# Weight sums of the first down part's twelve seven-product units: from VectorE sums staged in SBUF to accumulating transfers in HBM, with two signs turned

## The chip, the cores and the metric

The kernel runs on one core of one Trainium2 chip. The metric is the device time of one execution in microseconds (us). Before the change three runs took 1453.7, 1454.1 and 1455.69 us; the median is 1454.1 us.

## The reference

One decoder layer on 256 tokens of width 2048, all in float32: a mixer of two gated attention branches, then a gated feed-forward block with a short causal convolution. What matters here are the banded (sliding-window) attention of the mixer and the last product of the feed-forward block:

```python
s = jnp.einsum('bnqhgd,bnkhd->bhgnqk', q, kb) * SWA_HEAD_DIM ** -0.5     # banded attention, 32 query heads
s = jnp.where(mask, s + bias, -jnp.inf)                                  # bias by head and distance
...
def conv_ffn(h, w_up, conv_w, conv_b, w_down):                           # w_up 2048 x 11264, w_down 5632 x 2048
    a, b = jnp.split(h @ w_up, 2, axis=-1)
    ap = jnp.pad(a, ((0, 0), (CONV_WIDTH - 1, 0), (0, 0)))
    c = conv_b
    for j in range(CONV_WIDTH):
        c = c + conv_w[j] * ap[:, j:j + S]
    return (jax.nn.gelu(c, approximate=True) * b) @ w_down
```

## The kernel before, in words

**Products.** Every weight arrives by a transfer on SP's queue as a raw tile of 128x1024 float32 (512 KB), is split by ACT (line 163) and DVE (line 164) into a high and a low part, `whi` and `wlo`, and enters three matmuls (`mm3`, lines 197 to 200: high times high, high times low, low times high). A raw tile feeds twelve matmuls. Raw tiles and parts stand in rings of a few buffers; while a conversion is late, TensorE has only the parts already made.

**Seven-product units.** `pair_gemm` (line 273) makes a product over 1024 columns. Its letters "p" are plain units, its letters "s" units in which eight block products are replaced by seven (Strassen's scheme in Winograd's form, for two weight rows of 128, `even` and `odd`, and two halves of 512 columns). Such a unit needs four sums of weight blocks and four sums of token blocks (`token_sums`, line 375). With E0, E1 the halves of the even row and O0, O1 those of the odd row, the weight sums are E1-E0, O1-E1, then O1-(E1-E0), and O0 minus that.

**Parked sums.** `park_sums` (line 237) makes these sums early: `load` brings the two weight rows into SBUF by two transfers on POOL's queue (line 245), `even` and `odd` are four DVE subtractions of 128x512 (line 252), and two more POOL transfers store the result into two HBM tiles `td` (lines 257 and 262). `seven_parked` (line 300) later loads these tiles on SP's queue as if they were weights. `park_a` (line 269) is its use for the first down part (the first 24 of the 44 weight rows of 128, over both halves of the columns): `PAIR_ORDER` holds six "s" for each of the two products, twelve units in all, with tiles named `ta0` to `ta11` (in the profile `ta_s` in SBUF, `ta` in HBM). Four of them (`EARLY`, line 836) are made during the gate and output products behind the banded attention, eight (line 1376) during the up products. The same helper makes sums for other products (`tw`, `tb`, `tc`); these are not touched.

**Order of the work.** `at(t, f)` files a step under tick t and `tick()`, which the product loops call once for each raw tile or two, runs the steps that are due. The program text so made is then put in order for each engine by a scheduler, before the run; on the chip every engine and every transfer queue takes its instructions in that fixed order. POOL issues its transfers itself, so a POOL instruction that waits holds up all POOL instructions behind it.

**Banded attention.** From line 706 on, 16 units of two heads each go through the ticks, two ticks apart (`swa_unit`, line 625), between the matmuls of the projection of the queries. Unit u needs its bias tile, which POOL fetches out of a small HBM strip (line 633, two buffers: unit u's fetch waits until unit u-2 has used its own), at the DVE step of line 644, which adds it to the scores in PSUM. At the unit's end POOL makes the low part of the output (line 698). The tick counter is set to 0 just before (line 584). The first product of the kernel (`first_product`, line 501, about the first 50 us) comes ahead of it.

Of the kernel before, what the change touches and what calls it, by code (L numbers as in the profile page):

```python
# [11 lines left out]
F32 = mybir.dt.float32  # L12
# [4 lines left out]
ALU = mybir.AluOpType  # L17
# [25 lines left out]
def trunk_layer(ctx, tc, x, x_cols_in, conv_cols_in, g_mix_post, g_ffn_post, w_in, w_q, w_kv,  # L43
# [193 lines left out]
    def park_sums(name, w, k, c0, pl, tag, t0, bufs=None):  # L237

        td = [dram.tile([P, 1024], F32, name=f"{name}{i}") for i in range(2)]
        st = []  # L240

        def load():
            st.append(sb(pl, [P, D], f"{name}s", tag=tag, bufs=bufs))
            for i in range(2):
                ins = pool.dma_start(st[0][:, i * 1024:(i + 1) * 1024], w[(k + i) * P:(k + i + 1) * P, c0:c0 + 1024])
                if tag not in staged:
                    tc.keep_in_program_order(ins)
            staged.add(tag)

        def less(o, x, y):  # L250
            o, x, y = (st[0][:, i * 512:(i + 1) * 512] for i in (o, x, y))
            tc.keep_in_program_order(vec.tensor_tensor(o, x, y, op=ALU.subtract))

        def even():
            less(0, 1, 0)
            less(1, 3, 1)
            pool.dma_start(td[0], st[0][:, 0:1024])

        def odd():
            less(3, 3, 0)  # L260
            less(2, 2, 3)
            pool.dma_start(td[1], st[0][:, 1024:2048])

        at(t0 - 5, load)
        at(t0, even)
        at(t0 + 1, odd)
        return td

    def park_a(i, pl, tag, t0, **kw):
        u, p = (i, 0) if i < NA[0] else (i - NA[0], 1)  # L270
        return park_sums(f"ta{i}_", w_down, 2 * u, 1024 * p, pl, tag, t0, **kw)

    def pair_gemm(name, w, k0, c0, order, act_of, s_of, kind, d, place=None, sums=None, parked=None, held=None, into=None):

        c11, c12, c21, c22 = c = banks(kind, f"c{name}_")
        q, used = [], set()
        row = lambda k: w[(k0 + k) * P:(k0 + k + 1) * P, c0:c0 + 1024]
        half = lambda w_, i: tuple(x[:, i * 512:(i + 1) * 512] for x in w_)

        def mul(o, x, w_, last=False):  # L280
            mm3(o, *x, *w_, id(o) not in used, last)
            used.add(id(o))

        chunks, hold = [2 * order.count("p")], len(held) if held else 0
        left = [order.count("s")]

        def plain(u, last):
            for k in (2 * u, 2 * u + 1):
                chunks[0] -= 1
                w_ = convert(raw_row(row(k)), 1024, into=into(chunks[0]) if hold else None)  # L290
                for t in range(NT):
                    if t and chunks[0] < hold:
                        held[hold - 1 - chunks[0]] = (act_of(k, 1), w_)
                        continue
                    for j in range(2):
                        mul(c[2 * t + j], act_of(k, t), half(w_, j),
                            not (chunks[0] or (t and hold)) and (j == 1 or not left[0]))
                tick()

        def seven_parked(u, last):  # L300
            s1, s2, s3, s4 = s_of(u)
            if not q:
                q[:] = banks(1 - kind, f"q{name}_")
            q1, q5, q7, q6 = q
            w_ = convert(raw_row(row(2 * u + 1)), 1024)
            mul(c11, act_of(2 * u + 1, 0), half(w_, 0))
            mul(c12, s4, half(w_, 1))
            w_ = convert(raw_row(row(2 * u)[:, 0:512], 512), 512)
            mul(q1, act_of(2 * u, 0), half(w_, 0), last)
            w_ = convert(raw_row(parked[u][0]), 1024)  # L310
            mul(q5, s1, half(w_, 0), last)
            mul(q7, s3, half(w_, 1), last)
            tick()
            w_ = convert(raw_row(parked[u][1]), 1024)
            left[0] -= 1
            mul(q6, s2, half(w_, 1), last)
            mul(c21, act_of(2 * u + 1, 1), half(w_, 0))
            tick()
            if last:
                end_sums()  # L320

        def seven(u, last):
            s1, s2, s3, s4 = s_of(u)
            even, odd = place()
            pool.dma_start(even, row(2 * u))
            pool.dma_start(odd, row(2 * u + 1))
            ta, tb = sums()
            w_ = convert(odd, 1024)
            weight_sums(even, odd, ta, tb)
            if not q:  # L330
                q[:] = banks(1 - kind, f"q{name}_")
            q1, q5, q7, q6 = q
            mul(c11, act_of(2 * u + 1, 0), half(w_, 0))
            mul(c12, s4, half(w_, 1))
            w_ = convert(even, 512)
            mul(q1, act_of(2 * u, 0), half(w_, 0), last)
            w_ = convert(ta, 1024)
            mul(q5, s1, half(w_, 0), last)
            mul(q7, s3, half(w_, 1), last)
            tick()  # L340
            w_ = convert(tb, 1024)
            left[0] -= 1
            mul(q6, s2, half(w_, 0), last)
            mul(c21, act_of(2 * u + 1, 1), half(w_, 1))
            tick()
            if last:
                end_sums()

        def end_sums():
            q1, q5, q7, q6 = q  # L350
            d0, d1, d2, d3 = d() if callable(d) else d

            def first_sums():
                act.copy(d0, q1)
                vec.tensor_tensor(d1, d0, q6, op=ALU.add)
                vec.tensor_tensor(d2, d1, q7, op=ALU.add)

            def more_sums():
                vec.tensor_tensor(d3, d2, q5, op=ALU.add)
                vec.tensor_tensor(d1, d1, q5, op=ALU.add)  # L360

            at(now[0], first_sums)
            at(now[0] + 1, more_sums)

        n = order.count("s")
        plain_of, seven_of = iter(range(n, len(order))), iter(range(n))
        for i, kd_ in enumerate(order):
            if kd_ == "s":
                u = next(seven_of)
                (seven_parked if parked else seven)(u, u == n - 1)  # L370
            else:
                plain(next(plain_of), i == len(order) - 1)
        return c

    def token_sums(g, a, m, hi, lo):

        vec.tensor_tensor(a, g[:, 0:512], g[:, 512:1024], op=ALU.add)
        a11, a21, a12, a22 = (a[:, i * P:(i + 1) * P] for i in range(4))
        m1, m2, m3, m4 = (m[:, i * P:(i + 1) * P] for i in range(4))
        vec.tensor_tensor(m1, a21, a22, op=ALU.add)  # L380
        vec.tensor_tensor(m3, a11, a21, op=ALU.subtract)
        vec.tensor_tensor(m2, m1, a11, op=ALU.subtract)
        vec.tensor_tensor(m4, a12, m2, op=ALU.subtract)
        split_to(hi, lo, m)
        return [[x[:, i * P:(i + 1) * P] for x in (hi, lo)] for i in range(4)]

# [205 lines left out]
    OH, OL = pair_view(highs(ot)), pair_view(lows(ot))  # L592
    sb(base, [P, LINE_W], "line_w")

    qx_of, xs_of = {}, {}

    def swa_q(g, acc):
# [235 lines left out]
    out_b(0, tb[0], (pss, "s"))  # L833
    tb[1], tb[2] = gate_pair(1)
    parked_b2 = []
    parked_a = [park_a(i, pg, "gr", now[0] + 5 + 5 * i, bufs=2) for i in range(EARLY)]
    out_b(1, tb[1], (pss, "s"))
    tb[3] = gate_b(3)
    out_b(2, tb[2])
# [485 lines left out]
    def g_sums(u):  # L1325

        if u % 2 == 0:
            s_tiles[u // 2] = sums_tile("s", u // 2)
        hi, lo = (s_tiles[u // 2][:, (u % 2) * 1024 + i * 512:(u % 2) * 1024 + (i + 1) * 512] for i in range(2))
        a, m = (sb(s_pool[0], [P, 512], f"s{n}{u}", tag="hx", bufs=2) for n in "am")  # L1330
        s_of[u] = token_sums(gtiles[u].bitcast(F32), a, m, hi, lo)

    def gemm_cols(acc, c0):

# [37 lines left out]
            at(now[0] + 1 + 2 * i, lambda i=i: conv_cols(4 * c + i, sa[0][i], sa[1][i], slot0 + i))  # L1372

    es7 = ffn_up0()
    for i in range(sum(NA) - EARLY):
        parked_a.append(park_a(i + EARLY, t0=now[0] + 8 + 15 * i // 2, **STAGE))
    for c in range(1, 6):
        if c == 2:
            for i in range(8):
# [25 lines left out]
    for p in range(2):  # L1405
        d = [dsum[t][2 * p + j] for t in range(NT) for j in range(2)]
        c = pair_gemm(f"d{p}", w_down, 0, 1024 * p, PAIR_ORDER[p], lambda k, t: (GH(k)[:, t * P:(t + 1) * P], GL(k)[:, t * P:(t + 1) * P]),
                      lambda u: s_of[u], p, d, parked=parked_a[NA[0] * p:])
        for n_, (o, x_) in enumerate(zip(d, c)):
            at(now[0] + n_, lambda o=o, x_=x_: vec.tensor_tensor(o, o, x_, op=ALU.add))  # L1410
    more_raw.clear()
    turn.update(raw=0)
    sb_tiles = []
# [153 lines left out]
NB2 = B2_ORDER.count("s")  # L1567
W_ORDER = "ppspspsp"
PAIR_ORDER = ("pppspsspsssp", "ppspspsspssp")
EARLY = 4  # L1570
NA = [o.count("s") for o in PAIR_ORDER]
NB_ = B_ORDER.count("s")
XCUT = [0, 1, 2, 3, 4, 6, 8, 10, 12, 14, 16]
# [67 lines left out]
```

## Time and profile before

| What | Value |
|---|---|
| median of three runs | 1454.1 us |
| the profiled execution: its own time, its span | 1454.23 us, 1452.5 us |
| PE busy | 1442.0 us (99%) |
| DVE busy | 1160.4 us (80%) |
| POOL busy | 118.2 us (8%) |
| share of the 16 DMA engines taken by SP's queue, by POOL's queue | 59.8%, 15.0% |
| mean rate of all transfers | 248 GB/s |
| granted TensorE clock | 0.998 |

PE is TensorE's matmuls, PEld its weight loads, DVE VectorE, ACT ScalarE, POOL GpSimd, SP SyncE. Times in the views are microseconds from the start of the span. Matmuls overlap each other, so that "busy" says that TensorE has work, not how much of it; how long an engine waited for which other one stands in the view of waits. The first queue in the list of transfers (q1) is SP's, q0 is POOL's.

### The profile page before, as it was taken

Reading aid. Unit: us, or ns where it says so; the run is one execution under the profiler, and the core shown is the slowest. Engines: PE = TensorE matmul, PEld = TensorE weight load, DVE = VectorE, ACT = ScalarE, POOL = GpSimd, SP = SyncE. Lnnn points to the kernel's source line nnn. Section 1 sums busy time; section 2 is a strip of 40 time slices with the busy share of each in tenths; the row PEclk is TensorE's granted clock in tenths of the full one; section 3 lists DMA queues with packets and bytes.
Section 4 is the critical chain, followed back from the end, with each engine's and each line's share of the span. In section 5 each row is a group of like instructions: output and inputs, shape, how many; then the busy total and the mean of one; then the engine's idle time right before and its main releaser. Section 6 shows DMA issues by size and latency. Waiting matters only on the chain.

```text
span 1452.5 us, 21438 instructions
## 1 busy us (share of the span) xinstructions
PE 1442.0 (99%) x7518; PEld 1233.7 (85%) x7518; DVE 1160.4 (80%) x2056; ACT 864.7 (60%) x1422; POOL 118.2 (8%) x222
## 2 busy tenths in 40 slices
PE   9999999999999999999999999999999999999997
PEld 7888888888898888888888888888888888888886
DVE  7788896766878775888789899876777797987798
ACT  7588864544555655546566565655646565555673
POOL 2022110010000001100000111000000101000000
PEclk9999999999999999999999999999999999999999
DMA  8655376699875759965666898866878888789965
GB/s 309 209 171 163 103 261 188 219 327 294 244 220 178 230 164 319 348 232 183 219 205 208 272 331 288 292 206 210 310 276 262 312 276 292 246 265 309 340 219 203
DMA packets 164684, 359.69 MB, mean 248 GB/s; under 512 B 20816, under 2 KB 31952, under 8 KB 164576
## 3 DMA queue, kind: packets, MB, share of 16 engines
q1 hardware_dynamic: 143152, 282.49, 59.8%
q0 software_dynamic: 21280, 75.56, 15.0%
q8 instruction: 59, 0.97, 0.3%
q14 instruction: 49, 0.40, 0.1%
q10 hardware_dynamic: 144, 0.26, 0.1%
HBM read 323.62 MB, written 34.65 MB: 247 GB/s over the span
## 4 chain that ended last, share of the span: by engine, by line
PE 91%; DVE 4%; ACT 2%; DMA 2%; issue 1%; SPq 0%; DVEq 0%; ACTq 0%
PE ub L1340 10%; PE ua L1340 9%; PE accg L200 9%; PE accg L198 9%; PE accg L199 9%; PE ub L1344 5%; PE ua L1344 5%; PE cd L199 2%; PE cd L198 2%; PE cd L200 2%; DVE wlo L164 2%; DMA raw<-in_ffn_w_up_dram 1%; PE cdc L199 1%; PE cdc L198 1%; PE cdc L200 1%
## 5 line engine op out<-in xcount | busy, mean ns | idle before, releaser
L163 ACT CAST whi<-raw 128x1024 fp32r<-128x1024 f32 (+2 forms) x497 | 504.0, 1023 | 373.9 <-PE accg L200 109.1
L164 DVE TENSOR_TENSOR wlo<-raw,whi 128x1024 fp32r<-128x1024 f32 (+2 forms) x497 | 585.0, 1188 | 172.0 <-ACT whi L163 165.6
L198 PE MATMUL accg<-whi,ahl 128*128 128x512 f32 (+1 forms) x416 | 162.5, 391 | 0.0
L200 PE MATMUL accg<-whi,ahl 128*128 128x512 f32 (+1 forms) x416 | 160.7, 386 | 0.0
L199 PE MATMUL accg<-wlo,ahl 128*128 128x512 f32 (+1 forms) x416 | 159.8, 384 | 0.0
L1340 PE MATMUL ub<-ahl,whi 128*128 128x512 f32 x640 | 154.7, 391 | 0.2 <-DVE uu L1239 0.2
L1340 PE MATMUL ua<-ahl,whi 128*128 128x512 f32 x640 | 154.6, 391 | 0.0
L1340 PEld LDWEIGHTS ub<-ahl,whi 128*128 128x128 f32 x640 | 117.5, 188 | 23.1 <-ACT cc L1232 0.5
L1340 PEld LDWEIGHTS ua<-ahl,whi 128*128 128x128 f32 x640 | 117.6, 188 | 22.7
L198 PE MATMUL accg<-whi,bhl 128*128 128x512 f32 x256 | 100.8, 394 | 0.0
L200 PE MATMUL accg<-whi,bhl 128*128 128x512 f32 x256 | 100.0, 391 | 0.0
L199 PE MATMUL accg<-wlo,bhl 128*128 128x512 f32 x256 | 99.9, 390 | 0.0
L200 PEld LDWEIGHTS accg<-whi,ahl 128*128 128x128 f32 x416 | 78.1, 188 | 15.2
L199 PEld LDWEIGHTS accg<-wlo,ahl 128*128 128x128 f32 x416 | 78.3, 188 | 13.0
L198 PEld LDWEIGHTS accg<-whi,ahl 128*128 128x128 f32 x416 | 78.2, 188 | 12.9
L1344 PEld LDWEIGHTS ub<-ahl,wlo 128*128 128x128 f32 x640 | 82.2, 191 | 3.3
L1344 PEld LDWEIGHTS ua<-ahl,wlo 128*128 128x128 f32 x640 | 82.2, 191 | 3.1
L1344 PE MATMUL ua<-ahl,wlo 128*128 128x256 f32 x640 | 83.7, 283 | 0.0
L1344 PE MATMUL ub<-ahl,wlo 128*128 128x256 f32 x640 | 83.3, 283 | 0.0
L200 PEld LDWEIGHTS accg<-whi,bhl 128*128 128x128 f32 x256 | 48.1, 188 | 10.1
L199 PEld LDWEIGHTS accg<-wlo,bhl 128*128 128x128 f32 x256 | 48.1, 188 | 9.6
L198 PEld LDWEIGHTS accg<-whi,bhl 128*128 128x128 f32 x256 | 48.1, 188 | 9.6
(659 smaller groups left out, 2679.7 us busy)
## 6 DMA issues: line engine op xcount, KB each, us to landing
raw<-in_ffn_w_up_dram SPq DMA_DIRECT2D x142, 512.0 KB, 4.9
raw<-in_w_in_dram SPq DMA_DIRECT2D x105, 512.0 KB, 4.6
raw<-in_ffn_w_down_dram SPq DMA_DIRECT2D x66, 512.0 KB, 5.6
xraw<-in_ffn_w_up_dram SPq DMA_DIRECT2D x34, 512.0 KB, 5.2
raw<-in_w_o_swa_dram SPq DMA_DIRECT2D x32, 512.0 KB, 5.3
raw<-in_w_o_mla_dram SPq DMA_DIRECT2D x26, 512.0 KB, 6.9
raw<-in_w_out_dram SPq DMA_DIRECT2D x26, 512.0 KB, 4.6
ta_s<-in_ffn_w_down_dram POOLq DMA_DIRECT2D x24, 512.0 KB, 5.9
```

The costliest lines, as they stand in the source:

```text
L163: act.copy(hi[:, a:b], raw[:, a:b])
L164: vec.tensor_tensor(lo[:, a:b], raw[:, a:b], hi[:, a:b].bitcast(F32), op=ALU.subtract)
L198: pe.matmul(o, ah, bh, start=start, stop=False)
L199: pe.matmul(o, ah, bl, start=False, stop=False)
L200: pe.matmul(o, al, bh, start=False, stop=stop)
L1340: pe.matmul(acc[i], hi[:, c], hn[p][:, j * 512:(j + 1) * 512], start=p + j == 0, stop=stop)
L1344: pe.matmul(acc[i][:, 0:256], lo[:, c], hn[p][:, j * 512:j * 512 + 256], start=False, stop=False)
```

## The change

`park_a` no longer uses SBUF and DVE. A new helper, `park_sums_dma`, makes the four sums of a unit in the two HBM tiles by five transfers on POOL's queue, of which three accumulate (add what they read to what stands at their destination): the even row into the first tile and the left halves of both rows into the second; the right halves added to the first tile, which makes E0+E1 and E1+O1; the second half of that added to both halves of the second tile; and the even row's left half added to the second tile's second half. Since a transfer can add and not subtract, the sums have other signs than before; `token_sums` with `plus=1` turns the signs on the token side (one of its subtractions is now a scalar_tensor_tensor, as large as before), `seven_parked` with `plus=1` swaps two halves, and the four sums at the end of each product subtract where they added. The twelve units are filed from tick 1 on, two ticks apart, four ticks each, and their text stands ahead of the banded attention.

```diff
-    def park_a(i, pl, tag, t0, **kw):
+    def park_sums_dma(name, w, k, c0, t0):
+
+        td = [dram.tile([P, 1024], F32, name=f"{name}{i}") for i in range(2)]
+        by_row = [t.rearrange("p (a n) -> p a n", a=2) for t in td]
+        rows = w[k * P:(k + 2) * P, :].rearrange("(a p) n -> p a n", p=P)
+        left, right = (rows[:, :, c0 + i * 512:c0 + (i + 1) * 512] for i in range(2))
+
+        def copy():
+            pool.dma_start(td[0], w[k * P:(k + 1) * P, c0:c0 + 1024])
+            pool.dma_start(by_row[1], left)
+
+        at(t0, copy)
+        at(t0 + 1, lambda: pool.dma_start(by_row[0], right, accum_op=ALU.add))
+        at(t0 + 2, lambda: pool.dma_start(by_row[1], td[0][:, 512:1024].unsqueeze(1).to_broadcast([P, 2, 512]), accum_op=ALU.add))
+        at(t0 + 3, lambda: pool.dma_start(td[1][:, 512:1024], left[:, 0, :], accum_op=ALU.add))
+        return td
+
+    def park_a(i, t0):
         u, p = (i, 0) if i < NA[0] else (i - NA[0], 1)
-        return park_sums(f"ta{i}_", w_down, 2 * u, 1024 * p, pl, tag, t0, **kw)
+        return park_sums_dma(f"ta{i}_", w_down, 2 * u, 1024 * p, t0)
...
-            mul(q6, s2, half(w_, 1), last)
-            mul(c21, act_of(2 * u + 1, 1), half(w_, 0))
+            mul(q6, s2, half(w_, 1 - plus), last)
+            mul(c21, act_of(2 * u + 1, 1), half(w_, plus))
...
+        if plus:
+            vec.tensor_tensor(m1, a22, a21, op=ALU.subtract)
+            vec.scalar_tensor_tensor(m2, m1, -1.0, a11, op0=ALU.mult, op1=ALU.subtract)
+            vec.tensor_tensor(m4, a12, m2, op=ALU.add)
...
+    parked_a = [park_a(i, 1 + PARK_EVERY * i) for i in range(sum(NA))]
     qx_of, xs_of = {}, {}
...
-    parked_a = [park_a(i, pg, "gr", now[0] + 5 + 5 * i, bufs=2) for i in range(EARLY)]
...
-    for i in range(sum(NA) - EARLY):
-        parked_a.append(park_a(i + EARLY, t0=now[0] + 8 + 15 * i // 2, **STAGE))
...
-            at(now[0] + n_, lambda o=o, x_=x_: vec.tensor_tensor(o, o, x_, op=ALU.add))
+            at(now[0] + n_, lambda o=o, x_=x_, n_=n_: vec.tensor_tensor(o, x_, o, op=(ALU.add, ALU.subtract)[n_ % 2]))
...
-EARLY = 4
+PARK_EVERY = 2
```

In the changed file the five transfers stand at lines 277 and 278 (the two copies), 281 (right halves added), 282 (the half of the first tile added to the second) and 283 (the last half). The bias fetch moves from line 633 to 656, the strip's store from 448 to 470, the low part of the attention's output from 698 to 721, all without a change.

On POOL, behind the strip's store, this is the program of before: only bias fetches and low parts follow each other (the numbers in `bias0` and `bhl0_...<-o0` are those of the attention's units, the last number is a buffer's).

```order
L448 DMA strip_153<-strip_s_155 32x384
L633 DMA bias0_671<-strip_153 128x2x256
L633 DMA bias1_759<-strip_153 128x2x256
L633 DMA bias2_763<-strip_153 128x2x256
L633 DMA bias3_860<-strip_153 128x2x256
L633 DMA bias4_1016<-strip_153 128x2x256
L698 TENSOR_TENSOR bhl0_606<-o0_883,bhl0_606 128x256
```

In the changed program the same queue holds, between the fetches for attention units 1 and 2, the transfers of parked units 0 to 8; these are the last rows of them (`ta6_0` and `ta6_1` are the two HBM tiles of parked unit 6):

```order
L281 DMA ta6_0_627<-in_ffn_w_down_dram 256x1x512
L283 DMA ta5_1_626<-in_ffn_w_down_dram 128x512
L277 DMA ta7_0_629<-in_ffn_w_down_dram 128x1024
L282 DMA ta6_1_628<-ta6_0_627 256x1x512
L278 DMA ta7_1_630<-in_ffn_w_down_dram 256x1x512
L281 DMA ta7_0_629<-in_ffn_w_down_dram 256x1x512
L283 DMA ta6_1_628<-in_ffn_w_down_dram 128x512
L277 DMA ta8_0_631<-in_ffn_w_down_dram 128x1024
L656 DMA bias2_793<-strip_153 128x2x256
```

The fetch for attention unit 2 has moved behind the last transfer of parked unit 6. From there on one parked unit stands between one fetch and the next, up to the fetch for attention unit 7, behind the last transfer of the last parked unit:

```order
L656 DMA bias6_1231<-strip_153 128x2x256
L282 DMA ta11_1_638<-ta11_0_637 256x1x512
L721 TENSOR_TENSOR bhl1_607<-o2_1147,bhl1_607 128x256
L283 DMA ta11_1_638<-in_ffn_w_down_dram 128x512
L721 TENSOR_TENSOR bhl1_607<-o3_1257,bhl1_607 128x256
L656 DMA bias7_1341<-strip_153 128x2x256
L656 DMA bias8_1504<-strip_153 128x2x256
```

What moved here is only POOL's queue: the first copy of parked unit 0 stands even ahead of the making of the strip, and PE's, DVE's, ACT's and SP's instructions of the banded attention follow each other as before.

On DVE, during the second output product behind the attention, the sums stood between the conversions of before:

```order
L164 TENSOR_TENSOR wlo_3365<-raw_3362,whi_3364 128x1024
L252 TENSOR_TENSOR ta_s<-ta_s 128x512 x2
L164 TENSOR_TENSOR wlo_3389<-raw_3386,whi_3388 128x1024
L252 TENSOR_TENSOR ta_s<-ta_s 128x512 x2
L164 TENSOR_TENSOR wlo_3410<-raw_3407,whi_3409 128x1024
```

In the changed program the conversions stand alone:

```order
L164 TENSOR_TENSOR wlo_3438<-raw_3435,whi_3437 128x1024
L164 TENSOR_TENSOR wlo_3456<-raw_3453,whi_3455 128x1024
L164 TENSOR_TENSOR wlo_3474<-raw_3471,whi_3473 128x1024
L164 TENSOR_TENSOR wlo_3498<-raw_3495,whi_3497 128x1024
L164 TENSOR_TENSOR wlo_3516<-raw_3513,whi_3515 128x1024
```

All 48 DVE sums of line 252 on `ta_s` are gone; DVE has 1965 rows where it had 2006. On PE the matmuls are the same ones, in the same order but for a few rows within one up product.

More of the change, by code (lines that the diff above doesn't have):

```diff
@@ L267, in park_sums, with pair_gemm @@
         return td
-    def park_a(i, pl, tag, t0, **kw):
+    def park_sums_dma(name, w, k, c0, t0):
[12 more added lines that the diff above has]
+    def park_a(i, t0):
         u, p = (i, 0) if i < NA[0] else (i - NA[0], 1)
-        return park_sums(f"ta{i}_", w_down, 2 * u, 1024 * p, pl, tag, t0, **kw)
-    def pair_gemm(name, w, k0, c0, order, act_of, s_of, kind, d, place=None, sums=None, parked=None, held=None, into=None):
+        return park_sums_dma(f"ta{i}_", w_down, 2 * u, 1024 * p, t0)
+    def pair_gemm(name, w, k0, c0, order, act_of, s_of, kind, d, place=None, sums=None, parked=None, held=None, into=None, plus=0):
         c11, c12, c21, c22 = c = banks(kind, f"c{name}_")
@@ L373, in pair_gemm, with token_sums @@
         return c
-    def token_sums(g, a, m, hi, lo):
+    def token_sums(g, a, m, hi, lo, plus=0):
         vec.tensor_tensor(a, g[:, 0:512], g[:, 512:1024], op=ALU.add)
@@ L379, in token_sums @@
         m1, m2, m3, m4 = (m[:, i * P:(i + 1) * P] for i in range(4))
-        vec.tensor_tensor(m1, a21, a22, op=ALU.add)
         vec.tensor_tensor(m3, a11, a21, op=ALU.subtract)
-        vec.tensor_tensor(m2, m1, a11, op=ALU.subtract)
-        vec.tensor_tensor(m4, a12, m2, op=ALU.subtract)
+        if plus:
+            vec.tensor_tensor(m1, a22, a21, op=ALU.subtract)
+            vec.scalar_tensor_tensor(m2, m1, -1.0, a11, op0=ALU.mult, op1=ALU.subtract)
+            vec.tensor_tensor(m4, a12, m2, op=ALU.add)
+        else:
+            vec.tensor_tensor(m1, a21, a22, op=ALU.add)
+            vec.tensor_tensor(m2, m1, a11, op=ALU.subtract)
+            vec.tensor_tensor(m4, a12, m2, op=ALU.subtract)
         split_to(hi, lo, m)
@@ L1330, in g_sums @@
         a, m = (sb(s_pool[0], [P, 512], f"s{n}{u}", tag="hx", bufs=2) for n in "am")
-        s_of[u] = token_sums(gtiles[u].bitcast(F32), a, m, hi, lo)
+        s_of[u] = token_sums(gtiles[u].bitcast(F32), a, m, hi, lo, plus=1)
     def gemm_cols(acc, c0):
@@ L1407, in trunk_layer @@
         c = pair_gemm(f"d{p}", w_down, 0, 1024 * p, PAIR_ORDER[p], lambda k, t: (GH(k)[:, t * P:(t + 1) * P], GL(k)[:, t * P:(t + 1) * P]),
-                      lambda u: s_of[u], p, d, parked=parked_a[NA[0] * p:])
+                      lambda u: s_of[u], p, d, parked=parked_a[NA[0] * p:], plus=1)
         for n_, (o, x_) in enumerate(zip(d, c)):
-            at(now[0] + n_, lambda o=o, x_=x_: vec.tensor_tensor(o, o, x_, op=ALU.add))
+            at(now[0] + n_, lambda o=o, x_=x_, n_=n_: vec.tensor_tensor(o, x_, o, op=(ALU.add, ALU.subtract)[n_ % 2]))
     more_raw.clear()
```

## The prediction, made before the run

> **What bounds the kernel now.** The page first: its span, busy times and the chain that ended last.
>
> ```profile
> span 1452.5 us, 21438 instructions
> PE 1442.0 (99%) x7518; PEld 1233.7 (85%) x7518; DVE 1160.4 (80%) x2056; ACT 864.7 (60%) x1422; POOL 118.2 (8%) x222
> PE 91%; DVE 4%; ACT 2%; DMA 2%; issue 1%; SPq 0%; DVEq 0%; ACTq 0%
> ```
>
> TensorE has work in all but 10.5 us of the span. The view of waits for PE has three rows, of 1.7 us together:
>
> ```profile
> PE warm L76 <- DVE ramp L67: 1.1, 1, 1.1
> PE acckv L199 <- DVE wlo L164: 0.4, 1, 0.4
> PE ub L1340 <- DVE uu L1239: 0.2, 1, 0.2
> ```
>
> So a step taken off another engine pays only where TensorE waits for that engine. The view by windows, for the stretches from which work goes (250 to 350 and 800 to 950) and to which it comes (0 to 200); the columns are busy times, the granted clock, the DMA engines' share and GB/s:
>
> ```profile
> 0.00:110.00 110.00, 108.47 (x555) 91.05 (x556) 86.94 (x215) 80.25 (x168) 17.94 (x45) 1.00 0.72 229
> 110.00:200.00 90.00, 89.62 (x514) 77.15 (x513) 79.72 (x267) 80.87 (x214) 17.11 (x22) 1.00 0.51 147
> 250.00:350.00 100.00, 100.00 (x441) 82.38 (x440) 69.85 (x75) 46.99 (x49) 10.97 (x21) 1.00 0.81 270
> 800.00:950.00 150.00, 149.81 (x863) 132.23 (x862) 131.21 (x227) 88.08 (x141) 16.00 (x30) 1.00 0.87 295
> ```
>
> Where the sums are made today PE is busy 249.81 of 250 us. Where their replacement goes the DMA engines are taken for 72% of the first 110 us.
>
> **What is removed.** The view of the tile `ta_s`, all forms of it:
>
> ```profile
> L252 DVE TENSOR_TENSOR ta_s<-ta_s x48: 678/684/695, 290.5 to 936.6; 128x512 f32<-128x512 f32 x48
> L245 POOL DMA_DIRECT2D ta_s<-in_ffn_w_down_dram x24: 528/533/536, 258.4 to 926.6; - x24
> L257 POOL DMA_DIRECT2D ta<-ta_s x12: 532/537/539, 292.3 to 935.6; - x12
> L262 POOL DMA_DIRECT2D ta<-ta_s x12: 532/537/546, 295.0 to 937.6; - x12
> DMA to landing us min/median/max: 3.2/5.8/9.0
> ```
>
> 48 sums of 0.684 us are 32.8 us of DVE, and 48 transfers of 512 KB go from POOL's queue. All lie between 258 and 938 us, under a TensorE that has work; the most that they can give back is what it misses there, 0.2 us. I count them at -0.2. The turned signs cost nothing: `token_sums` has as many DVE steps of the same size as before (one form differs), and the sums at the ends of the products differ in sign alone. The loads of the parked tiles on SP's queue stay as they are.
>
> **What is added.** Sixty transfers on POOL's queue: 24 copies of 512 KB, and accumulating ones worth 30 times 512 KB (per unit 512, 512 and 256 KB). They are filed in a stretch in which POOL has little to do, but it is the queue that also fetches the bias tiles. POOL's timeline, the two ends of the gap that is filled and the fetch for attention unit 7:
>
> ```profile
> 10.42 0.51 POOL L448 DMA_DIRECT2D strip<-strip_s  x1 [0.31 <-POOL strip_s L447]
> 17.40 1.48 POOL L633 DMA_DIRECT2D bias<-strip  x2 [6.46 <-DMA strip<-strip_s]
> 62.38 0.72 POOL L633 DMA_DIRECT2D bias<-strip  x1 [43.51 <-DVE mx L646]
> ...
> 103.20 0.72 POOL L633 DMA_DIRECT2D bias<-strip  x1
> ```
>
> And DVE's timeline, where units 2 and 7 use theirs, with the landing of all 16 fetches from the view of the tile `bias`:
>
> ```profile
> 75.41 0.28 DVE L644 TENSOR_TENSOR p<-s,bias 128x128 f32<-128x128 f32 x1
> 115.67 0.28 DVE L644 TENSOR_TENSOR p<-s,bias 128x128 f32<-128x128 f32 x1
> DMA to landing us min/median/max: 3.5/4.4/6.9
> ```
>
> With a landing of 4.4 us the fetch for unit 2 must be issued by 71.0 us and that for unit 7 by 111.3. In the changed program seven parked units stand ahead of the first and all twelve ahead of the second. If a fetch is late, DVE stands at line 644; behind that in its order are the low parts of the weights (line 164), and TensorE waits for these. So what this costs is the time at which POOL reaches the fetch for unit 7, less 111.3 us. Two counts bound that time; the larger holds.
>
> *Count of waits.* An accumulating transfer must wait for the landing of what it adds to, and POOL waits with it. Followed back from the fetch for unit 7, each link to the landing that released it, there are 14 landings of accumulating transfers and 4 of copies, one behind the other. Some 12 us go before the first accumulating transfer can be issued (the strip's store is at 10.42), and some 14 for about two dozen issues on the way, at 0.53 to 0.72 us by the rows above. That makes 26 us and 18 landings. It meets 111.3 us only if a landing takes no more than 4.7 us. From the list of issues, transfers on POOL's queue of 512 KB, and loads in the stretch in which the chain begins:
>
> ```profile
> ta_s<-in_ffn_w_down_dram POOLq DMA_DIRECT2D x24, 512.0 KB, 5.9
> ta<-ta_s POOLq DMA_DIRECT2D x24, 512.0 KB, 5.5
> xr<-in_x_cols_dram SPq DMA_DIRECT2D x6, 256.0 KB, 8.4
> ```
>
> At 5.7 us each the fetch is issued at 128.6, 17 us late; at 9.0, the slowest `ta_s` landing, at 188, 77 us late.
>
> *Count of engine time.* The weights that TensorE needs up to there still have to come: 0.72 of 110 us is 79 us of all 16 engines. The price of POOL's transfers is on the page (packets, MB, share of the span):
>
> ```profile
> q0 software_dynamic: 21280, 75.56, 15.0%
> ```
>
> 15.0% of 1452.5 us for 75.56 MB is 2.88 us for a MB, 1.51 us for 512 KB. The copies take 24 x 1.51 = 36 us. The trace has no accumulating transfer. From below it costs as much as a plain one: 30 x 1.51 = 45 us, and 79 + 36 + 45 is 160 us, 49 too many. From above I take three plain ones, as if reading the addend, reading the old value and writing went one by one, each at the price of a whole transfer: 136 us, 140 too many. My value is 1.5 plain ones, since a plain transfer reads once and writes once and this one reads twice and writes once: 68 us, 183 in all, 72 too many. The Trainium skill (Collectives: The Full Stack, "The bandwidth ceiling") says that a transfer that adds is half as fast as a copy, because two sources are read through the same ring; by it the accumulating ones would take 91 us, and the delay would be 95. No run here shows it yet.
>
> **Sum.** -0.2 for what goes, +72 for the fetches, over the profiled execution's 1454.23 us, which is 0.1 above the median of the three runs: 1526 us. A part of the 72 will be seen earlier, as weights that come late in the first product, whose loads share the engines with the first parked units; it moves all that follows, and isn't added, since the late fetches are counted from the start of the span. Behind unit 7 POOL's queue is as it was, and the delay stays at what it is.
>
> **The rivals.**
> 1. *Copies and additions land fast* (chance 0.20). The engines work on several transfers at once better than the price on the page says, and the count of waits alone holds: +17, 1471 us; with accumulating ones at the price of plain ones up to +49, 1503 us. For it: the mean DMA share between 110 and 200 us is only 0.51. Against it: the 0.72 ahead of that, and the 8.4 us of the `xr` loads.
> 2. *From HBM to HBM is far slower* (0.20). No transfer of the trace both reads and writes HBM, and an addition whose reads and write go one by one gives the upper end: +140, 1594 us, or beyond. The Trainium skill (DMA: Bandwidth & Descriptors, "Latency and other measured facts") has copies between HBM tensors at 214 GB/s at best; by that the copies take 59 us, the additions, at 1.5, 110, and the delay is 137. The trace's price for POOL's plain transfers is 347 GB/s, with one end in SBUF.
> 3. *Not slower: POOL keeps pace* (0.08). POOL is busy for 8% of the span and stood still for 43.51 us ahead of the fetch for unit 2. If a landing in the chain takes 4.7 us or less, all fetches come in time, TensorE waits as little as now, and the time is 1454.2 less at most 0.2: no change. It decides at that landing of 4.7 us. The bias fetches, half as large, need 4.4; nothing of 512 KB on this queue has a median below 5.5 in the rows above, and 4 to 5 landings in the chain fall into the full first 40 us. A gain of over 0.2% would need 2.9 us, and the places from which work goes miss 0.2; I leave 0.02 of the 0.08 for it, for TensorE's other idle time.
>
> **How the numbers follow.** The forecast, +49 to +95 with +72 as its value, has 0.52. The range runs from the count of waits alone (+17, 1471) to additions at three plain transfers (+140, 1594); what lies outside are rival 3 and the far end of rival 2. A measurement of this kernel can tell about 0.2% (2.9 us) from no change. Faster by more: 0.02; within: 0.06; slower: 0.92.
>
> **What would show it.** Right: in the view of waits new rows of DVE at line 644 on a bias transfer, or of PE on the low parts of the weights, with some tens of us; the fetch for unit 2 (line 656) at some 100 us instead of 62, and that for unit 7 at some 180; the spacing of attention units 2 to 7 at 11 to 16 us where it is 8 today; `ta` transfers at lines 281 and 282 with landings of 8 to 10 us; a stretch behind unit 7 that is as long as before; DVE's busy time lower by 33 us and no stretch behind 250 us shorter. Wrong: landings under 4.7 us at lines 281 and 282, or fetches that are issued by 71 and 111 us. If TensorE waits in the first 60 us for nearly all of the delay and the fetches are in time for the work so moved, the engines are the bound and the queue's order isn't.

## The result and the profile after

The changed kernel took 1540.69 us, the median of five runs (1539.5 to 1544.2); the kernel before, run beside it, 1453.7 (1453.52 to 1455.69). The ratio is 1.0603 with a 95% interval of 1.0590 to 1.0615: 87 us slower. The forecast was 1526, its range 1471 to 1594.

The page of the changed kernel: span, busy times, granted clock in 40 slices, POOL's transfers, and the copies and first additions with their median landing.

```profile
span 1542.4 us, 21358 instructions
PE 1459.0 (95%) x7518; PEld 1243.6 (81%) x7518; DVE 1137.8 (74%) x2008; ACT 865.7 (56%) x1422; POOL 141.7 (9%) x234
PEclk9975899999999999999999999999999999999999
q0 software_dynamic: 26080, 78.71, 18.0%
ta<-in_ffn_w_down_dram POOLq DMA_DIRECT2D x36, 512.0 KB, 10.0
```

The span is 89.9 us longer, and the same 7518 matmuls show how: PE stands still for 83.4 us where it was 10.5 (+72.9), and is busy 17.0 us longer with the same work; the granted clock falls in the slices in which it starves. Added up over windows of 20 us up to 220 us, the busy time times the missing part of the clock is 16.5 us of these 17.0, an estimate by which the clock accounts for nearly all of them. To find the place, the view by windows after, cut at 200 us:

```profile
0.00:200.00 200.00, 125.36 (x564) 100.73 (x564) 91.54 (x223) 83.01 (x173) 66.35 (x105) 0.81 1.02 268
200.00:1542.00 1342.00, 1333.60 (x6955) 1142.86 (x6955) 1046.24 (x1786) 782.66 (x1249) 75.40 (x130) 1.00 0.70 230
```

The same view of before, cut 90 us earlier:

```profile
110.00:1452.00 1342.00, 1333.56 (x6965) 1142.62 (x6963) 1073.50 (x1842) 784.44 (x1255) 100.28 (x177) 1.00 0.76 249
```

The last 1342 us are alike: 1333.60 us of PE against 1333.56, at full clock. All 90 us are lost in the first 200, which do what 110 did before, with the 16 DMA engines taken throughout (share 1.02; the sum of the packets' times can go a little over 1). That behind it POOL and DVE have less to do shows nowhere in PE. Inside the first 200 us:

```profile
80.00:100.00 20.00, 14.78 (x81) 12.12 (x79) 9.02 (x29) 11.80 (x33) 5.26 (x6) 0.98 1.08 300
100.00:120.00 20.00, 0.00 (x0) 0.00 (x0) 0.00 (x0) 0.00 (x0) 5.54 (x7) 0.50 0.94 186
120.00:140.00 20.00, 0.00 (x0) 0.00 (x0) 1.20 (x7) 0.00 (x0) 7.75 (x9) 0.50 0.99 189
180.00:200.00 20.00, 11.44 (x47) 9.28 (x47) 12.14 (x38) 8.46 (x21) 6.26 (x9) 0.79 0.94 213
```

From 100 to 140 us no engine but POOL works (DVE for 1.2 us), the clock goes to 0.50, and the DMA engines are full all the same (0.94 and 0.99), nearly all of it with the parked units' transfers. The view of waits after, the longest rows of three engines that lie there and ACT's wait for raw weights up to 220 us, names who stands on whom:

```profile
PE pt L645 <- DVE o L719: 51.8, 3, 46.2
DVE p L667 <- DMA bias<-strip: 72.7, 5, 47.8
POOL ta L283 <- DMA ta<-ta: 53.2, 12, 7.7
POOL ta L282 <- DMA ta<-in_ffn_w_down_dram: 38.2, 10, 5.8
POOL ta L281 <- DMA ta<-in_ffn_w_down_dram: 20.8, 9, 4.4
ACT whi L163 <- DMA raw<-in_w_in_dram: 24.4, 13, 4.4
```

Read from the bottom up: weights come late (24.4 us; 5.3 before), POOL stands before each accumulating transfer until the one ahead has landed, DVE stands at the bias tile, once for 47.8 us, and PE stands for what DVE would have made behind it. Last, the line of the bias fetch on POOL, once in a window that holds the fetch for attention unit 2 alone and once in one that holds that for unit 7 (duration, first and last start), and the landings of the three accumulating lines 281, 282 and 283:

```profile
L656 POOL DMA_DIRECT2D bias<-strip x1: 1072/1072/1072, 128.8 to 128.8; - x1
L656 POOL DMA_DIRECT2D bias<-strip x1: 1051/1051/1051, 198.7 to 198.7; - x1
DMA to landing us min/median/max: 7.8/10.1/13.7
DMA to landing us min/median/max: 6.2/8.7/10.2
DMA to landing us min/median/max: 5.1/7.6/9.2
```

The fetch for unit 2 moved from 62.4 to 128.8 us and that for unit 7 from 103.2 to 198.7. It had to be issued by 111.3: 87.4 us late, and the kernel is 87 us slower. From 12 us up to that fetch POOL's timeline shows only waits of the chain itself, beside 4.8 us for the strip, and none for a step of the attention: the chain sets the time of the fetch.

### The profile page after: what moved, and what is told of

It is laid out like the page before. It is cut to its first block, busy times and chain, and to the rows that moved or that the text cites. A ratio compares the mean times of both kernels' runs of the same rounds, so it can differ in the third digit from the quotient of the medians.

```text
span 1542.4 us, 21358 instructions
## 1 busy us (share of the span) xinstructions
PE 1459.0 (95%) x7518; PEld 1243.6 (81%) x7518; DVE 1137.8 (74%) x2008; ACT 865.7 (56%) x1422; POOL 141.7 (9%) x234
## 4 chain that ended last, share of the span: by engine, by line
PE 52%; DMA 1%; DVE 0%; issue 0%; ACT 0%; DVEq 0%; ACTq 0%
PE ua L1362 9%; PE ub L1362 9%; PE ub L1366 5%; PE ua L1366 5%; PE cd L199 2%; PE cd L198 2%; PE cd L200 2%; PE accg L198 2%; PE accg L200 2%; PE accg L199 2%; PE cdc L199 1%; PE cdc L198 1%; PE cdc L200 1%; DMA mr1hi<-in_w_out_dram 1%; PE cdb L200 1%; PE cdb L199 1%
## 5 line engine op out<-in xcount | busy, mean ns | idle before, releaser
L198 PE MATMUL accg<-whi,ahl 128*128 128x512 f32 (+1 forms) x416 | 167.4, 403 | 4.5 <-DVE vx L442 4.5
L200 PE MATMUL accg<-whi,ahl 128*128 128x512 f32 (+1 forms) x416 | 164.7, 396 | 0.0
L199 PE MATMUL accg<-wlo,ahl 128*128 128x512 f32 (+1 forms) x416 | 164.0, 394 | 0.0
L198 PEld LDWEIGHTS accg<-whi,ahl 128*128 128x128 f32 x416 | 81.0, 195 | 18.6 <-issue 4.9
L200 PEld LDWEIGHTS accg<-whi,ahl 128*128 128x128 f32 x416 | 80.8, 194 | 16.3
L645 PE MATMUL pt<-ident,p 128*128 128x128 f32 x96 | 16.4, 303 | 63.3 <-DVE o L719 51.8
L667 DVE TENSOR_TENSOR p<-s,bias 128x128 f32<-128x128 f32 x32 | 9.2, 287 | 78.8 <-DMA bias<-strip 72.7
L645 PEld LDWEIGHTS pt<-ident,p 128*128 128x128 f32 x96 | 12.0, 153 | 67.7 <-DVE o L719 52.1
```

What stands on the lines that cost most here:

```text
L198: pe.matmul(o, ah, bh, start=start, stop=False)
L199: pe.matmul(o, ah, bl, start=False, stop=False)
L200: pe.matmul(o, al, bh, start=False, stop=stop)
L645: pe.transpose(pt[:, j * P:(j + 1) * P], p[:, c * P:(c + 1) * P], ident)
L667: vec.tensor_tensor(p[:, 0:P], sp[:, P:256], bias[:, 0:P][:, ::-1], op=ALU.add)
```

## The experiments

Two theories went in. **Queue**: POOL's in-order queue holds the attention's steps behind the chain of parked units. **Engine time**: the chain takes the DMA engines from the weights, wherever it stands in a queue. Ratios are to the kernel before on the same chip in the same session (medians 1453.9, 1453.5, 1453.7, 1453.4).

**1. The bias fetches on another queue** (`e1_bias_sp`).

```diff
-            pool.dma_start(st["bias"], bass.AP(strip.tensor, ...
+            nc.sync.dma_start(st["bias"], bass.AP(strip.tensor, ...
```

> The changed kernel, but the bias tiles of the banded attention are fetched on SP's queue instead of POOL's, so that no fetch stands behind a parked unit; the sixty transfers of the parked units stay as they are. Queue theory (the delay of 87 us is the time at which POOL's ordered queue reaches the fetch for unit 7): the fetches come in time, and what is left is the weights that come late beside the parked units, +15 to +30 us over the kernel before. Engine theory (the 16 DMA engines have too much to move until then, whatever the order): +45 to +65 us, now as waits for weights.

1543.49 us, ratio 1.0612 (1.0595 to 1.0630): no gain, and far above what either theory expected. Its waits:

```profile
DVE o L719 <- POOL bhl L721: 48.2, 3, 30.4
PE pt L645 <- DVE p L697: 32.4, 2, 31.1
ACT whi L163 <- DMA raw<-in_w_in_dram: 40.0, 18, 7.3
```

The bias tiles come in time now (DVE waits 6.5 us for them where it waited 72.7), and another step of the attention has taken their place. POOL makes the low part of each unit's output (line 721), that too stands behind the chain, the output tile has two buffers, and DVE stands at the third. So the run moved the wait and could not judge the theories. Run 5 takes both off POOL.

**2. Plain copies in place of the accumulating transfers** (`e2_plain`).

```diff
-        at(t0 + 1, lambda: pool.dma_start(by_row[0], right, accum_op=ALU.add))
+        at(t0 + 1, lambda: pool.dma_start(by_row[0], right))
```

and so in the other two.

> The changed kernel with the three accumulating transfers of each unit made plain copies of the same size (the weight sums are left out, so that the output is another one). In the changed kernel's trace an accumulating packet of 2 KB takes 178 ns and a plain one 84 ns. Engine theory: 30 transfers of 512 KB, 16 packets on each engine, 94 ns less each are 45 us less, so about +42 us over the kernel before. Queue theory: the same fourteen plus four landings one behind the other, of about 6.5 us where they are 8 to 9 now: +40 to +60 us. If an addition cost no more than a copy, nothing would change: +87.

1506.39 us, ratio 1.0368 (1.0350 to 1.0386): 52.5 us slower than before, 34 less than the change. That lies within what the queue theory expected and 10 us above what the engine-time theory did, too near to both to tell them apart; it does show that the adding lengthens the chain. DVE's wait for the bias is 40.2 us where it was 72.7:

```profile
DVE p L667 <- DMA bias<-strip: 40.2, 6, 24.6
```

And the fetch for unit 7, in a window that holds it alone:

```profile
L656 POOL DMA_DIRECT2D bias<-strip x1: 741/741/741, 161.9 to 161.9; - x1
```

161.9 less 111.3 is 50.6, and the cost is 52.5.

**3. POOL's order pinned** (`e3_kept`): all five transfers in `tc.keep_in_program_order(...)`, so that one parked unit stands between two bias fetches, where the scheduler had put seven ahead of the fetch for unit 2.

> The changed kernel with each of the sixty transfers pinned in POOL's order at the tick at which it is filed, so that one parked unit goes beside each unit of the banded attention instead of seven ahead of the third. Between two bias fetches there are then two accumulating landings one behind the other, and twelve parked units end beside attention unit 14. Engine theory: the engines have until unit 14 for the same work, +50 to +65 us. Queue theory: two landings of 7 to 8 us and 2 to 3 us of issues make the units 17 to 18 us apart where they were 8, twelve times: +100 to +120 us. A delay that begins only behind the first product is expected by both.

1548.08 us, ratio 1.0646 (1.0631 to 1.0662): 94 us, between what the two expected and nearer to the queue theory. The last five fetches on POOL:

```profile
L656 POOL DMA_DIRECT2D bias<-strip x5: 1095/1247/1263, 215.9 to 268.2; - x5
```

And DVE's waits for all of them:

```profile
DVE p L667 <- DMA bias<-strip: 94.1, 11, 13.9
```

The last fetch is at 268.2 us where it was 167.4. Eleven waits of 8.6 us on the mean take the place of five, of which one was 47.8 us long: the attention now goes at the pace of one parked unit for each of its own, with some 18 us from fetch to fetch. In twelve pieces the chain costs about as much as in one (94 us against 87).

**4. The signs alone** (`e4_signs`): the kernel before with DVE additions in its parked units and the signs turned as in the change.

> The kernel before with the turned signs alone: the weight sums are made on VectorE and parked as before, but as additions, and the token sums and the four sums at the ends of the products turn the signs. Both theories: the same time as the kernel before, within 0.2%.

1454.0 us, ratio 1.0001 (0.9992 to 1.0010). They cost nothing.

**5. Nothing of the attention on POOL** (`e6_ctrl` from the kernel before, `e6_free` from the one after).

```diff
-            pool.dma_start(st["bias"], ...
+            nc.sync.dma_start(st["bias"], ...
...
-            pool.tensor_tensor(OL(u), st["o"], OH(u).bitcast(F32), op=ALU.subtract)
+            vec.tensor_tensor(OL(u), st["o"], OH(u).bitcast(F32), op=ALU.subtract)
```

> The kernel before with two edits that empty POOL's queue of the attention's work: the bias fetch of an attention unit is issued by SP, and the low part of its output (128x256, 1.05 us on POOL) is computed on DVE. No parked unit is changed. It is the base for the run with the same two edits in the kernel after. Queue theory and engine-time theory both expect the time of before within 5 us (1449 to 1459): 16 low parts on DVE are some 16 x 0.4 = 6 us of DVE, which is busy some 18 of 20 us there, and the fetches keep their place in time. Above 1460 would mean that DVE in the attention has no room for them.

1453.51 us, ratio 1.0003 (0.9993 to 1.0012), as expected: the two edits are free by themselves.

> The kernel after with the same two edits, so that nothing of the attention stands on POOL behind the twelve parked units; all 60 transfers, their order and their waits stay. Queue theory (POOL's in-order queue holds back the attention, the transfers as such are nearly free): within 20 us of its base, 1450 to 1475, and the fetches of bias and the low parts at the times of before. Engine-time theory (the transfers take time of the 16 DMA engines from the weights; some 36 us of copies and 66 us of accumulating beside 105 us of other traffic up to 160 us): 1484 to 1520, with TensorE's waits at the first product's conversion (weights late) and none at the attention's. Both apply in part if it comes out between 1475 and 1484.

1493.67 us, ratio 1.0274 (1.0259 to 1.0290): 40 us over its base, within what the engine-time theory gave, and 47 us less than the change. Three windows of `e6_free`:

```profile
20.00:40.00 20.00, 12.10 (x43) 8.78 (x41) 7.61 (x12) 7.58 (x12) 4.36 (x6) 0.83 1.07 341
80.00:100.00 20.00, 15.08 (x66) 12.08 (x65) 7.66 (x20) 6.44 (x13) 5.57 (x7) 0.83 1.05 277
100.00:120.00 20.00, 20.00 (x112) 17.11 (x111) 18.03 (x62) 18.09 (x49) 6.03 (x7) 1.00 1.08 315
```

Its waits, ACT's for raw weights up to 220 us and one of POOL's:

```profile
ACT whi L163 <- DMA raw<-in_w_in_dram: 44.1, 21, 8.1
POOL ta L283 <- DMA ta<-ta: 66.3, 12, 7.7
```

The same row of its base, `e6_ctrl`:

```profile
ACT whi L163 <- DMA raw<-in_w_in_dram: 8.1, 6, 3.4
```

The chain is as slow as ever (POOL's wait at line 283 is even longer), and from 100 to 200 us TensorE is busy for 97 of 100 us beside it, with the engines' share still at 1.06 to 1.08. What it loses, it loses nearly all in the first 100 us, where the weights of the first products come late (44.1 us against 8.1): by 100 us it has done the 310 matmuls that its base has done by about 65. On the chain that ended last stand four landings of these weights, of 15.6 to 19.0 us, one behind the other; the median landing of these weights before was 4.6. So the queue theory's range, up to 1475, did not hold, and yet both causes are there: 47 of the 87 us go when the attention leaves POOL's queue, and the 40 that stay are engine time taken from weights that are due at once.

**6. The same, with plain copies** (`e9_free_plain`): `e6_free` with the three edits of run 2.

> The run with the attention off POOL's queue (1493.7 us, 40 over its base), with its 36 accumulating transfers as plain copies: the parked units hold copies and no sums, so the output is not the reference's. A plain packet of 2 KB took 84 ns, an accumulating one 178, so the chain takes some 33 us less of the engines' time, and of what is left of the delay (40 us) that much of it goes that falls in the first 100 us, about half of the chain: 1468 to 1483. If accumulating had no part in it: 1490 to 1496. If the delay were due to accumulating alone: 1453 to 1458.

1478.05 us, ratio 1.0170 (1.0155 to 1.0186), as expected. Of the 40 us of engine time 16 come from the adding, and 24 are left when all sixty transfers are plain. The page has POOL's transfers (for their price, see below):

```profile
q0 software_dynamic: 20960, 74.51, 14.0%
```

ACT's wait for weights, 44.1 us in run 5, goes along:

```profile
ACT whi L163 <- DMA raw<-in_w_in_dram: 32.0, 18, 5.9
```

**7. Four units in place of twelve** (`e7_four`): units 0 to 3 by transfers where the change has them, eight by DVE as before. In the four, two halves of a sum stand exchanged, so the kernel's result is another one; the work is the same.

> Only the first four of the twelve parked units are made by accumulating transfers, in the same place as in the kernel after; the other eight by DVE's additions as before, signs turned in all. Four units end on POOL at about 4 + 4 x 14 = 60 us, ahead of 71.0 us, when the fetch of attention unit 2 must be issued. Queue theory: no delay of a fetch, 1453 to 1459. Engine-time theory, in which the cost is in proportion to the transfers: 4/12 of 87 us, 1475 to 1490.

1472.49 us, ratio 1.0126 (1.0109 to 1.0143): 19 us, between the two and near the engine-time theory's lower end. ACT's wait for weights up to 220 us:

```profile
ACT whi L163 <- DMA raw<-in_w_in_dram: 28.6, 15, 4.2
```

The bias fetch for unit 2 (line 659 in this kernel):

```profile
L659 POOL DMA_DIRECT2D bias<-strip x1: 772/772/772, 86.4 to 86.4; - x1
```

Four units took POOL to 86 us and not to 60: beside the first products' weights a unit costs about 20 us and not 14. A third of the units costs a little under a quarter of 87 us, nearly all as late weights: DVE's wait for a bias tile, which came to 72.7 us in the change, is 2.7 us here.

**8. Twelve units behind the attention** (`e8_spread`): pinned, from tick 34 on, a unit each eight ticks, four ticks between its steps.

> All twelve units by accumulating transfers, but pinned in the order of the program and filed from step 34 on, one unit each 8 steps and four steps from one transfer of a unit to the next, so behind the last bias fetch, through the gate, output and latent products, where the share of the DMA engines was 0.6 to 0.95 before. Queue theory and engine-time theory both expect the time of before within 6 us (1450 to 1460), since by then nothing on POOL is due within a landing and the 100 us of engine time are spread over some 400 us. That the accumulating transfers cost as such, wherever they stand: 1480 or more.

1491.83 us, ratio 1.0257 (1.0222 to 1.0293): 38 us slower, where no cost was expected from either theory. Its longest waits of PE and one of DVE:

```profile
PE qg L199 <- DVE wlo L164: 20.4, 1, 20.4
PE qn L925 <- DVE qt L777: 6.5, 1, 6.5
DVE gta L230 <- DMA gr<-in_w_in_dram: 32.7, 3, 22.6
```

The fetches that DVE waits for:

```profile
L342 POOL DMA_DIRECT2D gr<-in_w_in_dram x3: 1042/1097/1183, 198.4 to 267.8; - x3
```

That is the queue again, at a place that I had not looked at: the gate product's own weight sums get their rows through POOL (line 342), pinned between parked units, and the third pair comes at 267.8 us where before it was at 242.4. The low part that PE waits for (20.4 us) is that of these sums. The rest of the 38 us I did not trace.

**9. Twelve units behind those fetches too** (`e9_slack`): from tick 80 on, nine ticks apart.

> All twelve units by accumulating transfers, pinned in the order of the program as in the spread run, but filed from step 80 on, behind the last weight fetch of the gate sums on POOL, one unit each nine steps (some 35 us) and four steps from one transfer to the next. If the spread run was slow because its gate weights stood in POOL's queue behind parked units (third fetch at 268 us in place of 242 before, DVE waiting 22.6 us for one): 1452 to 1462. If accumulating transfers cost by themselves wherever they stand, in proportion to their engine time: 1480 to 1495, as in the spread run.

1517.25 us, ratio 1.0444 (1.0422 to 1.0466): worse, and beyond both ends. Its longest waits of PE and DVE:

```profile
PE mT L1061 <- DVE lta L1087: 38.5, 1, 38.5
DVE lta L1087 <- DMA lyb<-yb_d: 41.9, 1, 41.9
```

Two pairs of fetches of the output product on POOL, the first of `lta` and the late one of `lyb`, each in a window that holds it alone:

```profile
L1069 POOL DMA_DIRECT2D lta<-ta_d x2: 566/570/574, 545.6 to 546.7; - x2
L1070 POOL DMA_DIRECT2D lyb<-yb_d x2: 1064/1076/1088, 663.2 to 663.8; - x2
```

The same lines of before:

```profile
L1047 POOL DMA_DIRECT2D lta<-ta_d x2: 542/544/546, 544.6 to 546.1; - x2
L1048 POOL DMA_DIRECT2D lyb<-yb_d x2: 542/543/544, 594.1 to 594.9; - x2
```

One run, two halves. Up to 545 us, with the first units made between 305 and 545, the program is 1.0 us behind. Five units are finished by then; the other seven end between 554 and 678 us, most of them back to back on POOL, the `lyb` fetch among them is 69 us late, and PE stands for 38.5 us. The transfers are of the same kind in both halves, but they stand closer in the second, where the engines' share is 0.98 against 0.91; so this run alone doesn't part the queue from the engine time, though the longest wait is one for a fetch in the queue.

**10. The first four of them alone** (`e10_four_slack`): run 7's four units at run 9's place, eight by DVE.

> The four units of the run that cost 19 us at the head of the program, made by the same twenty transfers, but pinned behind the gate products' weight fetches on POOL (about 305 to 430 us of the span), four steps from one transfer to the next; the other eight by DVE's additions. Place theory (a transfer costs what is queued behind it on POOL and what its engine time takes from weights that are due; in the run with all twelve there the first seven moved the fetch at 544.6 us by only 1 us): 1452 to 1457. If a unit made in this way costs some 5 us wherever it stands: 1470 to 1475.

1453.79 us, ratio 1.0003 (0.9994 to 1.0013): the time of before. POOL still waits, and nobody waits for POOL; POOL's row is followed by PE's longest wait behind 100 us and ACT's for the first weights:

```profile
POOL ta L283 <- DMA ta<-ta: 25.4, 3, 11.5
PE ms L965 <- ACT xr L905: 0.7, 1, 0.7
ACT whi L163 <- DMA raw<-in_w_in_dram: 6.5, 7, 1.7
```

The engines have no room to spare there. The view by windows where most of the twenty transfers go:

```profile
300.00:340.00 40.00, 40.00 (x178) 33.13 (x177) 19.05 (x17) 16.83 (x17) 7.68 (x10) 1.00 0.97 287
340.00:380.00 40.00, 39.26 (x201) 33.25 (x200) 26.95 (x41) 17.71 (x23) 7.14 (x10) 1.00 1.00 293
380.00:420.00 40.00, 40.00 (x257) 36.05 (x256) 33.16 (x70) 21.96 (x42) 8.18 (x12) 1.00 0.96 284
```

With a share of 0.96 to 1.00 TensorE is busy for 119.26 of 120 us. The same twenty transfers cost 19 us at the head of the program and nothing here.

**11. The removed work alone** (`e5_nosums`): the kernel before without any sums for the twelve units.

> The kernel before without any weight sums for the first down part: no DVE subtractions (48 of 0.68 us), none of the 48 transfers by POOL that loaded and stored them; the seven-product units read raw weight rows in their place, of the same shape, so the output is not the reference's. It is the removed part of the change alone. Prediction: 0.2 us less than before, so 1453 to 1455. If DVE's additions and their traffic did hold TensorE up somewhere, it would be 1449 or less.

1454.54 us, ratio 1.0006 (0.9997 to 1.0016). Not even leaving the sums out altogether makes the kernel faster. So another placement of the transfers isn't likely to gain anything either: the best that was measured is the time of before, for four units, in run 10.

## Why the prediction was right, and where its sizes were off

*What goes gives 0.2 us; the signs nothing.* Runs 11 and 4 agree: both show no change, though 0.2 us is less than they can tell.

*The fetches for units 2 and 7 come late, DVE stands at the bias and TensorE behind it.* This was right, with the waits at the lines named, though both fetches came later than the prediction's signs had them (128.8 us against some 100, 198.7 against some 180). "What this costs is the time at which POOL reaches the fetch for unit 7, less 111.3 us" gave 87.4 against 87 for the change and 50.6 against 52.5 with plain copies. As a cause it is only partly shown. When the attention leaves POOL, 40 of the 87 us stay, and then the attention is late because its matmuls are, not for a fetch (DVE waits 4.5 us for bias tiles in run 5). The prediction took late weights for an early view of the same delay ("isn't added"). That fits the change itself, where the late fetch accounts for the whole delay; run 5 shows them as a cost that stays when the late fetch is mended. It also named the bias fetch alone as what waits behind the chain; the low parts on the same queue hold the attention just as long (run 1).

*Count of waits.* It gave +17 at 5.7 us a landing and +77 at 9.0. The landings were 10.1, 8.7 and 7.6 us at the median for the three lines; 9.0 was the nearer end, not 5.7. The two plain copies of a unit landed in 8.9 and 10.2 us, and 18 landings of 9.6 us would make the whole 198.7. The `ta_s` landings of before came from a stretch with the engines at 0.81 to 0.87 and with plain packets.

*Count of engine time.* This is the term that was mis-sized. By the page after, POOL's transfers take 18.0% of 1542.4 us, 277.6 us. Those of before took 217.9, of which 72.5 were for the 25.2 MB removed (70 by run 11, in which they are left out). So the chain takes 132 us; less 36 for the copies, 96 are left for the accumulating ones, against 45 at the price of plain ones: 2.1 times. In run 5 (16.8% of 1491.4 us against 13.8% of 1451.4 in its base) it is 1.9 times. Runs 5 and 6 differ in the adding alone, and POOL's transfers take 44 us less in run 6, as much again as the plain price of 45. I took 1.5 (68 us). With 96 the count is 79 + 36 + 96 - 111.3 = +100, and +87 was measured. The Trainium skill (Collectives: The Full Stack, "The bandwidth ceiling") has the adding steps of a collective at about half the speed of its copying steps. Taken over to these transfers it made the sum +95, 8 us from the measured delay, and the trace agrees with that price. The forecast of +72 was 15 us off; that it came so near is partly luck, since the price was 28 us too low and the count at the measured price goes 13 us past the result.

*Rival 1, fast landings:* it fell by the landings. *Rival 2, HBM to HBM far slower:* it fell. In run 6 the chain is plain, and 14.0% of 1475.3 us less what remains of its base (200.3 - 72.5) is 79 us for 28.3 MB, 2.8 us for a MB, as for transfers with an end in SBUF (2.88). That is some 360 GB/s by engine time. The Trainium skill's 214 (DMA: Bandwidth & Descriptors, "Latency and other measured facts"), which it gives for copies from other queues, didn't hold for these. *Rival 3, no change:* it fell in this place, and came true for four of the twelve units in another (run 10).

*"A stretch behind unit 7 that is as long as before":* right, 1333.60 against 1333.56 us of PE. DVE's busy time fell by 22.6 us where 33 was expected; even with the sums left out altogether it fell by just 27.1 (1133.3 us in run 11). The rows of the 48 sums add up to 32.9 us, and by form no other group of DVE's differs between the two by more than 0.3 us. The records of steps that follow each other overlap at their ends (the sum at 290.54 us starts before the conversion of 289.40, 1.23 us long, has ended), and the busy time counts such time once, so that it falls by less than the steps that go.

What stays open: how 47 and 40 divide in the change itself, since there both waits overlap, and why the measured delay is 13 us under the count of engine time at the right price. The matmuls in the traces, of which a few can be missing, give a hint on the first. By 100 us the changed kernel has done 385, which the kernel before has done by 79: it is 21 us behind, and `e6_free`, whose loss nearly all falls there, is some 35 behind its base. By 86 us the changed kernel and run 7, which ends 19 us late, have both done 338. So in the change itself nearer 20 than 40 us are lost to late weights ahead of the long wait for the bias tile. On the second, the share of 1.02 makes 198.7 us hold 203 us of engine time, still 8 short of the 211 counted.

## What to carry to other kernels

Work moved off a busy engine pays only if the bound engine waits for it; here even dropping it was worth nothing, so the best possible result was "no change". A chain of dependent transfers on an in-order queue holds up whatever is queued behind it until its end: before putting one there, list every later instruction of that queue with its due time, compute steps as well as fetches, and not just in the stage in view (runs 1, 8 and 9 each found another one). And what a transfer costs depends on what is due beside it, which the share of the DMA engines doesn't tell: the same twenty cost 19 us beside weights that were due at once, and nothing where the engines were nearly as full (0.96 to 1.00) but TensorE went without a wait for them.

## What the runs showed of the hardware

- An accumulating transfer took 1.9 to 2.1 times the engine time of a plain one of the same bytes; copies from HBM to HBM took 2.8 us of all 16 engines for a MB, as much as loads and stores (2.88).
- With TensorE idle from 100 to 140 us the granted clock was 0.50, and 0.74 to 0.91 in the broken stretches up to 200 us; the same matmuls took 17 us longer, 16.5 of them by the estimate from the clock.
- With the DMA engines' share at 1.05 to 1.09 TensorE was full in one place (100 to 120 us of `e6_free`) and starved in another (20 to 100 us). In run 10 TensorE was full at 0.96 to 1.00. In these runs a full share did not tell who waits.
- POOL's own issue took 1.04 us at the median for the first accumulating line, and 0.65 for the same line as a plain copy (run 2). The copies of the changed kernel took longer to issue too: 0.85 and 1.19 us against 0.55 and 0.79 in run 2.
